# A conv-FFN layer on one core: gelu and gating product through a PSUM bank

## The chip, the cores and the metric

The kernel runs on one core of a Trainium2 chip. A core has a matrix engine (TensorE, PE in the rows), three engines for elementwise work (VectorE, DVE; ScalarE, ACT; GpSimd, POOL), and SyncE (SP), which here issues the DMAs. All working data lie in SBUF; matmul results go to PSUM, eight banks of 128 partitions x 512 fp32 values. TensorE, VectorE and ScalarE reach PSUM in this kernel; GpSimd works on SBUF alone. The metric is device time of one execution in microseconds, as a median of runs.

## The reference

One layer of a hybrid diffusion backbone, in fp32, for 512 latent tokens of width 1024. A token mixer comes first (retention, pooling, gates, output projection, layer norm); the change is in the second half, a gated MLP with a 3x3 depthwise convolution over the 8 x 64 token grid:

```
h = (u @ w_up)                       # 1024 -> 2 x 2816
h = depthwise_conv3x3(h) + conv_b    # over the 8 x 64 grid, per channel
a, b = split(h)                      # 2816 channels each
out = (gelu(a) * b) @ w_down         # 2816 -> 1024
x = post_norm(alpha * x + g2 * out)
```

## The kernel before

Every fp32 matmul operand is split into a high half (a rounded fp32r copy, by ScalarE) and a low half (the operand minus that copy, `sub`, L84, by VectorE or GpSimd), and each product is three matmuls: high x low, high x high, low x high (`mm3`, L93 to L96).

**Up projection.** The 2 x 2816 channels are 44 features of 128 channels, the two halves interleaved, so that feature 2f is the 128 channels of `a` and feature 2f + 1 those of `b` that they are multiplied with: 22 pairs. The loop at L1000 goes over the features. A feature is 8 x 3 = 24 matmuls of 512 columns into one PSUM bank (`feature_mm`, L383). For the first six features the first half of the tokens has been multiplied earlier, while the stage before was ending (`first_half`, L887), so that six banks are taken at the start. The weights of feature i + 2 are loaded and split while feature i is worked on (`up_prep`, L953): the high half by a ScalarE cast, the low half by GpSimd. There are three sets of buffers for them: two of `hi`, `lo`, and every third feature (i % 3 = 2) uses `spare`, parts of the slots that will hold the activations; such matmuls print `ps<-S,S`, the others `ps<-S,hi` and `ps<-S,lo`.

A finished feature is then convolved into an accumulator in SBUF (`accs[i]`, one of eight `t2` buffers). ScalarE writes bias and centre tap from the bank (L1010). Two of the other eight taps are scaled by ScalarE (L1013) and added by GpSimd (L936). The other six are done by VectorE, one instruction each, which reads the bank, the accumulator and a scale per partition (L938); three of feature i are woven with the last three of feature i - 1 (L1015 to L1018). The last two features are first copied out of their banks (L1005).

When both features of a pair are done, ScalarE applies the gelu in place (`gelu`, L983), VectorE multiplies with the other accumulator in place (`gated`, L986), ScalarE casts the product to its high half and VectorE subtracts for the low half (`act_out`, L989). All of these read and write SBUF. The halves are kept for the down projection.

**Down projection.** It runs over f = 0 to 21, each f being 24 matmuls, and accumulates four token blocks x two halves in all eight PSUM banks (`banks`, L1031). The first two f are done on six banks first (L1045). Weights are split as before; the low halves of f = 1 and of every second later f, f = 3 among them, are VectorE's (`down_prep`, L958). When it is done, gates, residual and norm follow.

**What sets the order.** From L922 on SyncE's instructions stay in the written order. For the other engines a planner orders the instructions, by its own estimate of times and by their place in the program, and gives each tile a free buffer of its kind as its use begins; a buffer comes free with the last instruction that uses it. On the chip each engine works through its list in order and waits for semaphores. The PSUM banks are one pool of eight (`bank`, L80).

Of the kernel before, what the change touches and what calls it, by code (L numbers as in the profile page):

```python
# [9 lines left out]
F32 = mybir.dt.float32  # L10
F32R = mybir.dt.float32r
AF = mybir.ActivationFunctionType
ALU = mybir.AluOpType
# [9 lines left out]
NFF = 2816 // P  # L23
# [23 lines left out]
def layer_kernel(ctx: ExitStack, tc: tile.TileContext, a: dict):  # L47
    nc = tc.nc
    act, dve, pool, pe, dma = nc.scalar, nc.vector, nc.gpsimd, nc.tensor, nc.sync
# [7 lines left out]
    def nm(s):  # L57
        count[0] += 1
        return f"{s}_{count[0]}"

    def slot(i, shape, dt=F32):
        return sb.tile(shape, dt, tag=f"S{i}", name=nm(f"S{i}"))
# [17 lines left out]
    def bank():  # L80
        return ps_pool.tile([P, SEQ], F32, tag="ps", name=nm("ps"))

    def sub(eng, out, x, y):
        eng.tensor_tensor(out, x, y, ALU.subtract)  # L84
# [839 lines left out]
    acts = [slot(s, [P, 8, SEQ], F32R) for s in (2, 7, 6, 5, 3, 0)]  # L924
# [44 lines left out]
    srcs, accs = {}, {}  # L969
# [6 lines left out]
    def weave(*gens):  # L976
        gens = list(gens)
        while gens:
            for g in list(gens):
                if next(g, 0) == 0:  # L980
                    gens.remove(g)

    def gelu(f):  # L983
        act.activation(accs[2 * f], accs[2 * f], AF.Gelu_apprx_tanh)

    def gated(f):  # L986
        dve.tensor_tensor(accs[2 * f], accs[2 * f], accs[2 * f + 1], ALU.mult)  # L987

    def act_out(f):  # L989
        hi = acts[f // 8][:, f % 8, :]  # L990
        act.copy(hi, accs[2 * f])
        sub(dve, acts[3 + f // 8][:, f % 8, :], accs[2 * f], hi.bitcast(F32))

    def settle(i):
        if i >= 0 and i % 2 == 0:
            gelu(i // 2)
        elif i >= 0:
            gated(i // 2)

    for i in range(2 * NFF):  # L1000
        up_prep(i + 2)
        ps = up_mm(i)
        if i >= 2 * NFF - 2:
            src = t2()
            act.copy(src, ps)  # L1005
        else:
            src = ps
        srcs[i] = src
        acc = accs[i] = t2()
        act.activation(acc, src, AF.Identity, bias=convb[:, i:i + 1], scale=convw[:, i, 4:5])  # L1010
        for n in POOL_TAPS:
            hs = t2()
            act.activation(hs, src, AF.Copy, scale=convw[:, i, n:n + 1])  # L1013
            tap(acc, hs, None, *TAPS[n])
        gens = [conv_taps(i, DVE_TAPS[:3])]  # L1015
        if i:
            gens.insert(0, conv_taps(i - 1, DVE_TAPS[3:]))
        weave(*gens)  # L1018
        settle(i - 1)
        if i >= 3 and i % 2 == 1:  # L1020
            act_out((i - 3) // 2)
    down0 = down_prep(0, pool)
    i = 2 * NFF - 1
    weave(conv_taps(i, DVE_TAPS[3:]))
    settle(i)
    act_out(NFF - 1)

    g2 = load(row(), gates[1:2, :].broadcast_to([P, D]))
# [176 lines left out]
```

## Time and profile before

| | us |
|---|---|
| median of 3 runs | 873.96 |
| lowest, highest run | 870.28, 1165.45 |
| the profiled execution | 874.79 |
| its span, first to last instruction | 873.0 |
| TensorE busy | 821.6 |
| VectorE busy | 624.4 |
| ScalarE busy | 366.2 |
| GpSimd busy | 444.2 |

The median is near the two lower runs. The profile is one execution, of 874.79 us; all rows below come from it, and their times count from the start of its span. Matmuls overlap, so that one lasts longer (0.39 us) than the distance between two starts.

### The profile page before, as it was taken

What the parts mean: (1) busy time and instruction counts of PE and PEld (TensorE: products, weight loads), DVE (VectorE), ACT (ScalarE), POOL (GpSimd) and SP (SyncE); (2) the same over time, 40 slices, a digit from 0 to 9 for tenths busy, and PEclk for the clock granted to TensorE, in tenths of its full rate; (3) what the DMA queues carried; (4) which work ended last, traced back from release to release, by engine and by line L of the source; (5) the groups of instructions that cost most, each with busy time, mean ns of one, the idle gap of its engine ahead of it and who ended that gap; (6) DMA issues with size and microseconds to landing.
All of it is one profiled execution on the core that took longest, in us unless ns stands there. A gap on an engine that the chain in (4) does not pass through costs nothing.

```text
span 873.0 us, 10556 instructions
## 1 busy us (share of the span) xinstructions
PE 821.6 (94%) x3865; PEld 678.5 (78%) x3865; DVE 624.4 (72%) x959; ACT 366.2 (42%) x575; POOL 444.2 (51%) x304
## 2 busy tenths in 40 slices
PE   6889989999999999998998899999999998799993
PEld 4667878778888888887787898888888776688883
DVE  7899996676267773346757769999999999612138
ACT  4434544121444343233335476666655565223200
POOL 4877411121543230113456878899888886212245
PEclk9999999999999999999999999999999999999997
DMA  9932466767221104344503312222222252224202
GB/s 352 345 105 94 127 207 218 236 226 216 72 73 49 50 1 145 100 154 163 196 1 121 121 50 84 86 96 99 96 97 95 75 169 83 87 97 144 73 1 96
DMA packets 33780, 106.94 MB, mean 122 GB/s; under 512 B 4528, under 2 KB 5312, under 8 KB 33728
## 3 DMA queue, kind: packets, MB, share of 16 engines
q1 hardware_dynamic: 33728, 106.27, 35.6%
q8 instruction: 30, 0.49, 0.2%
q14 instruction: 22, 0.18, 0.1%
HBM read 104.14 MB, written 2.11 MB: 122 GB/s over the span
## 4 chain that ended last, share of the span: by engine, by line
PE 40%; DVE 39%; POOL 8%; DMA 6%; issue 5%; ACT 2%; SPq 0%; DVEq 0%; POOLq 0%; ACTq 0%
DVE t L938 19%; PE ps L96 11%; PE ps L95 11%; PE ps L94 11%; DVE S L84 4%; DMA raw<-in_wada 4%; DVE t L987 3%; POOL lo L84 3%; DVE raw L203 2%; DVE lo L84 2%; PE ps L339 1%; POOL S L84 1%; POOL sm L123 1%; PE ps L608 1%; DVE sm L130 1%
## 5 line engine op out<-in xcount | busy, mean ns | idle before, releaser
L96 PE MATMUL ps<-S,lo 128*128 128x512 f32 (+1 forms) x544 | 212.2, 392 | 5.1 <-DVE lo L84 4.7
L94 PE MATMUL ps<-S,hi 128*128 128x512 f32 (+1 forms) x544 | 213.6, 393 | 2.7 <-ACT hi L89 2.7
L95 PE MATMUL ps<-S,hi 128*128 128x512 f32 (+1 forms) x544 | 212.5, 391 | 0.2 <-POOL S L84 0.2
L84 POOL TENSOR_TENSOR lo<-raw,hi 128x1024 fp32r<-128x1024 f32 (+1 forms) x53 | 134.0, 2530 | 107.2 <-ACT hi L89 105.3
L938 DVE SCALAR_TENSOR_TENSOR t<-ps,convw,t 128x441 f32<-128x441 f32 (+1 forms) x252 | 167.6, 693 | 15.8 <-POOL t L936 11.5
L89 ACT CAST hi<-raw 128x1024 fp32r<-128x1024 f32 (+1 forms) x98 | 98.9, 1009 | 168.2 <-PE ps L95 61.7
L96 PEld LDWEIGHTS ps<-S,lo 128*128 128x128 f32 x544 | 102.8, 189 | 29.8 <-DVE lo L84 6.8
L94 PEld LDWEIGHTS ps<-S,hi 128*128 128x128 f32 x544 | 103.6, 190 | 23.7 <-ACT hi L89 3.1
L936 POOL TENSOR_TENSOR t<-t,t 128x448 f32<-128x448 f32 x88 | 116.7, 1329 | 10.0 <-ACT t L1013 6.2
L95 PEld LDWEIGHTS ps<-S,hi 128*128 128x128 f32 x544 | 103.7, 191 | 21.3 <-POOL S L84 0.6
L95 PE MATMUL ps<-S,S 128*128 128x512 f32 (+1 forms) x308 | 113.8, 370 | 5.4 <-DVE S L84 5.0
L94 PE MATMUL ps<-S,S 128*128 128x512 f32 (+1 forms) x308 | 113.1, 369 | 3.6 <-DVE t L938 3.6
L96 PE MATMUL ps<-S,S 128*128 128x512 f32 (+1 forms) x308 | 113.8, 370 | 0.2 <-POOL S L84 0.2
L84 DVE TENSOR_TENSOR lo<-raw,hi 128x1024 fp32r<-128x1024 f32 (+1 forms) x47 | 61.4, 1307 | 53.0 <-ACT hi L89 53.0
L84 POOL TENSOR_TENSOR S<-raw,S 128x1024 fp32r<-128x1024 f32 x21 | 50.8, 2423 | 68.7 <-ACT S L735 44.5
L95 PE MATMUL ps<-lo,S 128*128 128x512 f32 x208 | 81.6, 392 | 0.7 <-DVE lo L84 0.6
L96 PE MATMUL ps<-hi,S 128*128 128x512 f32 x208 | 81.3, 391 | 0.0
L94 PE MATMUL ps<-hi,S 128*128 128x512 f32 x208 | 79.2, 392 | 0.0
L95 PEld LDWEIGHTS ps<-S,S 128*128 128x128 f32 x308 | 58.9, 191 | 15.6 <-DVE S L84 5.5
L94 PEld LDWEIGHTS ps<-S,S 128*128 128x128 f32 x308 | 58.6, 191 | 13.6 <-DVE t L938 4.0
L96 PEld LDWEIGHTS ps<-S,S 128*128 128x128 f32 x308 | 58.9, 191 | 10.4 <-POOL S L84 1.1
L84 POOL TENSOR_TENSOR S<-t,S 128x512 fp32r<-128x512 f32 (+1 forms) x29 | 44.8, 1557 | 31.2 <-DVE t L220 11.1
(205 smaller groups left out, 1187.3 us busy)
## 6 DMA issues: line engine op xcount, KB each, us to landing
raw<-in_w_up SPq DMA_DIRECT2D x44, 512.0 KB, 3.3
raw<-in_wada SPq DMA_DIRECT2D x32, 512.0 KB, 4.2
raw<-in_w_down SPq DMA_DIRECT2D x22, 512.0 KB, 3.3
S<-in_wada SPq DMA_DIRECT2D x16, 512.0 KB, 6.8
raw<-in_w_first SPq DMA_DIRECT2D x8, 512.0 KB, 7.4
raw<-in_w_v SPq DMA_DIRECT2D x16, 256.0 KB, 3.3
raw<-in_w_ga SPq DMA_DIRECT2D x8, 512.0 KB, 3.4
raw<-in_w_gb SPq DMA_DIRECT2D x8, 512.0 KB, 3.3
```

The lines of the kernel that those rows point to most:

```text
L84: eng.tensor_tensor(out, x, y, ALU.subtract)
L89: act.copy(hi, raw)
L94: pe.matmul(out, lhsT=sh, rhs=mh, start=first, stop=False)
L95: pe.matmul(out, lhsT=sh, rhs=ml, start=False, stop=False)
L96: pe.matmul(out, lhsT=sl, rhs=mh, start=False, stop=last)
L123: pool.tensor_scalar(rs, mv[:, 1:2], EPS, None, ALU.add)
L130: dve.bn_stats(st[:, hf, :], src[:, hf * SEQ:(hf + 1) * SEQ])
L203: dve.scalar_tensor_tensor(out_junk, raw, 1.0, silu_c, ALU.mult, ALU.mult, accum_out=mod[:, j:j + 1])
L339: pe.matmul(g0[f], lhsT=w[:, f * P:(f + 1) * P], rhs=m[:, kt, :], start=kt == 0 and i == 0, stop=kt == NKT - 1 and i == 2)
L936: pool.tensor_tensor(o, o, i, ALU.add)
L938: dve.scalar_tensor_tensor(o, i, w, o, ALU.mult, ALU.add)
L987: dve.tensor_tensor(accs[2 * f], accs[2 * f], accs[2 * f + 1], ALU.mult)
```

## The change

The gelu writes its result to a PSUM bank, not back to the accumulator in SBUF; the product is formed in place in that bank; the cast and the subtraction read it there. The last pair keeps its accumulator in SBUF. Nothing else is changed.

```diff
+    prod = {}
+
     def gelu(f):
-        act.activation(accs[2 * f], accs[2 * f], AF.Gelu_apprx_tanh)
+        prod[f] = accs[2 * f] if f == NFF - 1 else bank()
+        act.activation(prod[f], accs[2 * f], AF.Gelu_apprx_tanh)
 
     def gated(f):
-        dve.tensor_tensor(accs[2 * f], accs[2 * f], accs[2 * f + 1], ALU.mult)
+        dve.tensor_tensor(prod[f], prod[f], accs[2 * f + 1], ALU.mult)
 
     def act_out(f):
         hi = acts[f // 8][:, f % 8, :]
-        act.copy(hi, accs[2 * f])
-        sub(dve, acts[3 + f // 8][:, f % 8, :], accs[2 * f], hi.bitcast(F32))
+        act.copy(hi, prod[f])
+        sub(dve, acts[3 + f // 8][:, f % 8, :], prod[f], hi.bitcast(F32))
```

## Rows read from the trace of the kernel before

**Rows 1.** The page: busy time by engine; the chain that ended last, by line.

```profile
PE 821.6 (94%) x3865; PEld 678.5 (78%) x3865; DVE 624.4 (72%) x959; ACT 366.2 (42%) x575; POOL 444.2 (51%) x304
...
DVE t L938 19%; PE ps L96 11%; PE ps L95 11%; PE ps L94 11%; DVE S L84 4%; DMA raw<-in_wada 4%; DVE t L987 3%; POOL lo L84 3%; DVE raw L203 2%; DVE lo L84 2%; PE ps L339 1%; POOL S L84 1%; POOL sm L123 1%; PE ps L608 1%; DVE sm L130 1%
```

**Rows 2.** Stretches: length, busy us (x starts) of PE, PEld, DVE, ACT, POOL; clock, DMA.

```profile
720.30:732.00 11.70, 8.97 (x37) 6.42 (x35) 11.28 (x16) 5.46 (x8) 8.31 (x6) 1.00 0.27 90
732.00:743.70 11.70, 10.42 (x39) 8.44 (x40) 11.49 (x13) 6.64 (x10) 7.63 (x5) 0.85 0.27 91
743.70:755.40 11.70, 6.66 (x27) 5.00 (x26) 11.10 (x13) 2.84 (x4) 2.43 (x1) 0.95 0.00 0
```

**Rows 3.** Timeline, TensorE: start, us, line, operation; in brackets idle before, releaser.

```profile
527.66 0.39 PE L94 MATMUL ps<-S,S 128*128 128x512 f32 x1
...
674.54 0.39 PE L94 MATMUL ps<-S,S 128*128 128x512 f32 x1
...
726.11 0.39 PE L94 MATMUL ps<-S,S 128*128 128x512 f32 x1
...
733.28 0.50 PE L94 MATMUL ps<-S,S 128*128 128x512 f32 x1 [3.62 <-DVE t L938]
...
754.50 0.80 PE L95 MATMUL ps<-S,S 128*128 128x512 f32 x1 [5.04 <-DVE S L84]
...
761.10 0.39 PE L94 MATMUL ps<-hi,S 128*128 128x512 f32 x1
```

**Rows 4.** Timeline, VectorE: early, one steady pair, the end.

```profile
536.52 0.68 DVE L987 TENSOR_TENSOR t<-t,t 128x512 f32<-128x512 f32 x1
...
616.17 5.66 DVE L938 SCALAR_TENSOR_TENSOR t<-ps,convw,t 128x441 f32<-128x441 f32 x8
621.93 1.38 DVE L987 TENSOR_TENSOR t<-t,t 128x512 f32<-128x512 f32 x1
623.23 2.94 DVE L938 SCALAR_TENSOR_TENSOR t<-ps,convw,t 128x441 f32<-128x441 f32 x4
626.08 1.87 DVE L84 TENSOR_TENSOR S<-t,S 128x512 fp32r<-128x512 f32 x1
627.87 2.67 DVE L938 SCALAR_TENSOR_TENSOR t<-ps,convw,t 128x441 f32<-128x441 f32 x4
...
753.23 1.22 DVE L84 TENSOR_TENSOR S<-raw,S 128x1024 fp32r<-128x1024 f32 x1
754.37 0.68 DVE L987 TENSOR_TENSOR t<-t,t 128x512 f32<-128x512 f32 x1
```

**Rows 5.** Timeline, GpSimd: in the steady pair, and near the end.

```profile
624.99 2.41 POOL L84 TENSOR_TENSOR lo<-raw,hi 128x1024 fp32r<-128x1024 f32 x1 [0.67 <-ACT hi L89]
627.35 2.85 POOL L936 TENSOR_TENSOR t<-t,t 128x448 f32<-128x448 f32 x2
...
735.34 2.38 POOL L936 TENSOR_TENSOR t<-t,t 128x448 f32<-128x448 f32 x2 [5.86 <-ACT t L1013]
```

**Rows 6.** VectorE by line (count | busy us, mean ns | idle): 505-757, then whole.

```profile
L84 DVE TENSOR_TENSOR S<-t,S 128x512 fp32r<-128x512 f32 x22 | 33.7, 1530 | 0.7 <-ACT S L991 0.7
L987 DVE TENSOR_TENSOR t<-t,t 128x512 f32<-128x512 f32 x22 | 29.1, 1324 | 1.3
...
L743 DVE TENSOR_TENSOR S<-ps,S 128x512 f32<-128x512 f32 x8 | 5.5, 691 | 14.7 <-PE ps L96 14.7
...
L84 DVE TENSOR_TENSOR t<-t,t 128x512 fp32r<-128x512 f32 x4 | 2.7, 684 | 0.0
```

**Rows 7.** The same view, ScalarE, 490 to 770 us.

```profile
L1010 ACT ACTIVATE t<-ps,convb,convw 128x512 f32<-128x512 f32 x42 | 32.5, 773 | 3.3 <-PE ps L96 3.3
...
L984 ACT ACTIVATE t<-t 128x512 f32<-128x512 f32 x22 | 13.9, 634 | 43.2 <-DVE t L938 43.2
L991 ACT CAST S<-t 128x512 fp32r<-128x512 f32 x22 | 13.7, 622 | 51.1 <-DVE t L987 51.1
...
L1005 ACT COPY t<-ps 128x512 f32<-128x512 f32 x2 | 1.2, 576 | 0.0
```

## The prediction

> **What bounds the kernel now.** I read the page first, then the table of stretches, then TensorE's timeline, then VectorE's and GpSimd's. The page shows TensorE busy for 94% of the span, but the chain that ended last spends 19% of the span on VectorE's taps at L938 [rows 1]: both engines are near a limit, in different stages. Single stretches tell where. In 720 to 755 us, the end of the up projection and the start of the down projection, TensorE is busy 8.97, 10.42 and 6.66 us of 11.70, starts 37, 39 and 27 matmuls, and its granted clock falls to 0.85 and 0.95; VectorE is busy at least 11.10 of 11.70 in all three [rows 2].
>
> TensorE's own timeline gives its rate and its loss. Features are told apart by their weights: every third (8, 11, 14, ...) has weights in the spare slots and prints `ps<-S,S`. Feature 8 begins at 527.66 and feature 35 at 674.54: 27 features of 24 matmuls in 146.88 us, 0.2267 us each and 5.44 us a feature, with no wait in them [rows 3]. From feature 35 to the down projection's f = 4 (761.10) there are 9 x 24 + 4 x 24 = 312 matmuls, which at that rate take 70.7 us; the rows show 86.6. So **TensorE loses 15.8 us** there, and this is all that a faster up projection can give back: from 527 to 674 it waits for nothing, and behind 761 the change touches nothing. [...]
>
> That pace: one pair of features costs VectorE eight taps, the product, four taps and the low-half subtraction, with no gap; from 616.17 to the next group at 627.87 (1.79 us after the subtraction began) is 11.70 us [rows 4]. TensorE needs 2 x 5.44 = 10.88. VectorE falls 0.8 us a pair behind, and at the end it pays: its last product starts at 754.37 [rows 4], while TensorE finished the up projection at 726.11 [rows 3].
>
> **What the change does, part by part.**
>
> The product and the subtraction. Today both read two SBUF operands: 1.38 and 1.87 us in the steady pair, but 0.68 us for the same product at 754.37 [rows 4], when GpSimd has nothing to do. The wait is for GpSimd: the subtraction begun at 626.08 ends at 627.95, 0.6 us after GpSimd's next instruction could begin (627.35), and GpSimd's two taps take 2.85 us there against 2.38 with nothing in their way at 735.34 [rows 5]. The taps read one operand from PSUM and one from SBUF and keep 0.72 us apart whatever GpSimd does [rows 4]. So an operand in PSUM should end the wait on both sides. Price of the subtraction after: no row has this exact form; the nearest are 0.684 us (two SBUF operands, undisturbed) and 0.691 us (a bank and SBUF, L743, same size) [rows 6]; I take 0.69, upper bound today's mean 1.53. The product writes its result to the bank as well; nothing but TensorE writes PSUM in this trace, so its bounds are 0.69 and today's mean 1.32; I take 0.69, since its reads are those of L743. Over the phase VectorE saves 33.7 - 22 x 0.69 = 18.5 us on subtractions and 29.1 - 22 x 0.69 = 13.9 us on products [rows 6], 32.4 in all (the last pair, which stays as it is, already costs 0.69). A pair falls from 11.70 to about 9.8 us, under TensorE's 10.88.
>
> [...]
>
> GpSimd. Its pair is two weight subtractions of 2.41 and four taps; the taps fall from 2.85 to 2.38 a pair of them [rows 5], so 9.6 us instead of 10.5. It is hidden under TensorE's 10.88, closely: if its waits for the weight casts stayed, it would be the next to bound a pair, at about 11.
>
> ScalarE. The gelu writes a bank: 0.634 us now, bounds 0.576 (a copy out of a bank) and 0.773 (bias and scale out of a bank); the high-half cast (0.622) reads a bank instead: 0.576 to 0.77 [rows 7]. I take no change; at worst 21 x 0.3 = 6 us, which its 43 and 51 us of waiting ahead of these two lines cover [rows 7]. If that cover went, the bias line behind the gelu would come late, and with it GpSimd's and VectorE's taps.
>
> Buffers. The SBUF accumulator is free some 10 us earlier; nothing waits long for it, so nothing is gained. One PSUM bank of eight is taken from the gelu to the end of the subtraction. No DMA, weight or matmul is added or moved. SyncE keeps its written order; the planner orders the other engines and will plan them anew, which the trace of before cannot show.
>
> **The sum.** VectorE's last work would end at 755.1 - 32.4 = 722.7 us if it never starved. TensorE without waits ends the up projection at 674.54 + 9 x 5.44 = 723.5. So VectorE catches up just as TensorE finishes, and then waits for feature 43: copy 0.58, bias 0.77, one scaled copy of like cost, two GpSimd taps 2.4, nine taps at 0.72, product and subtraction, about 12 us (an estimate from rows 4 to 7): done near 736. TensorE needs f = 3's low half at 723.5 + 72 x 0.2267 = 739.8: in time. [...] I leave 3 us of the 15.8: the product bank of f = 20 and the tap bank of feature 41 come free a few us after 723.5, while the down projection wants all eight banks, and f = 1's low half also stands in VectorE's queue. The profiled execution took 874.79 us (span 873.0), 0.8 above the median of 873.96. 874.8 - 15.8 + 3 = **862 us**.
>
> **Rivals.**
>
> *Early banks.* Feature 9 begins at 527.66 + 5.44 = 533.1, while the second product (features 2 and 3) starts only at 536.52 [rows 3, 4]: features 3 to 9 hold seven of eight banks. A product bank makes eight; if two overlap, TensorE must fall back by one or two features, 5.4 to 10.9 us, less what VectorE's faster start gives: 866 to 872. For: seven are full. Against: VectorE saves 2 to 4 us in exactly these first pairs.
>
> *Slower: the gelu waits for a bank.* ScalarE works in order; a gelu that waits for a bank holds back the weight cast and bias behind it, so GpSimd, VectorE and then TensorE. It decides from 1.85 us a pair on (11.70 - 9.85): then VectorE's gain is gone, and TensorE has lost two features early (10.9) and 0.15 x 11.7 = 1.8 us at the lower clock, as in the stretch from 732 [rows 2]: 874.8 + 12.7 = 887; with longer waits more. Against: in the steady pair the product's bank would be given back (627.95) before the next gelu. [...]
>
> *It doesn't do what it says.* If a product that reads and writes a bank still waits for GpSimd, the subtraction alone saves 18.5 us and most of the gain stays; if neither is freed, 873 to 876. Against: the taps.
>
> *More than I count.* All 15.8 us plus a low run: under 857.
>
> **How the numbers follow.** Forecast (858 to 866) 0.66; early banks 0.12; no effect 0.08; gelu waits 0.09; more 0.05. The range 856 to 874 leaves out about half of "more", half of "no effect" and the slower case, some 0.16. 2% of 873.96, about what such a measurement tells from no change, is 17.5 us: faster means under 856.5, which is 18 us below the profiled run and above the 15.8 that can be had, so 0.06; slower means over 891.4, the far end of the gelu case, 0.04; the rest 0.90.
>
> **What would show it.** Right: product and subtraction near 0.69 us while GpSimd is busy; GpSimd's tap pairs at 2.4; TensorE's matmuls 0.227 us apart through 685 to 760 with no long wait and no fall of the clock; f = 4 of the down projection some 12 us earlier; everything from there as before. Wrong: waits of matmuls on VectorE around 515 to 560; ScalarE's gelu waiting for something other than its last tap; a VectorE pair of 11.7 us still; or f = 3 waiting as now.

## The result: slower by a tenth

The changed kernel takes 967.80 us (median of four runs, 965.47 to 969.16) against 873.96 before: a ratio of 1.108 (95% interval 1.106 to 1.110). The forecast was 862 with a range of 856 to 874, and slower by over 2% had a chance of 0.04. The profiled span is 967.4 us, so 94.4 us more than before.

The page after: busy time by engine, then the chain that ended last by line.

```profile
PE 851.1 (88%) x3865; PEld 691.5 (71%) x3865; DVE 604.1 (62%) x959; ACT 364.6 (38%) x575; POOL 425.8 (44%) x304
...
PE ps L96 10%; PE ps L95 10%; PE ps L94 10%; POOL t L936 8%; POOL lo L84 7%; POOL S L84 4%; DVE t L938 4%; DMA raw<-in_wada 3%; DVE raw L203 2%; DVE lo L84 2%; PE ps L339 1%; POOL sm L123 1%; DVE S L84 1%; PE ps L608 1%; DVE S L226 1%
```

VectorE, ScalarE and GpSimd are each busy for **less** time than before (604.1, 364.6 and 425.8 us against 624.4, 366.2 and 444.2 [rows 1]), and the kernel is slower. What the products and subtractions were to save was saved (the next rows), so the loss is waiting. In the chain GpSimd's lines (taps L936, weight low halves L84) have come in, and VectorE's taps have gone from 19% to 4%.

VectorE and ScalarE by line, 500 to 870 us (count | busy us, mean ns | idle before, releaser), to set beside [rows 6, 7]:

```profile
L990 DVE TENSOR_TENSOR ps<-ps,t 128x512 f32<-128x512 f32 x21 | 14.7, 699 | 1.9
L84 DVE TENSOR_TENSOR S<-ps,S 128x512 fp32r<-128x512 f32 x21 | 14.5, 691 | 12.4 <-ACT S L994 12.4
L987 ACT ACTIVATE ps<-t 128x512 f32<-128x512 f32 x21 | 12.6, 602 | 87.1 <-DVE t L938 87.0
L994 ACT CAST S<-ps 128x512 fp32r<-128x512 f32 x21 | 12.3, 586 | 95.9 <-DVE ps L990 95.9
```

Product and subtraction cost 0.70 and 0.69 us, as predicted. But ScalarE now stands still for 87 us ahead of the gelus and 96 us ahead of the casts, where it was 43 and 51 [rows 7]. No gelu waits for a bank: all of its wait is for VectorE's last tap of its own pair.

One pair of features after, ScalarE, then GpSimd, then VectorE (start, us, line, operation; in brackets the idle time before, and its releaser):

```profile
616.09 0.59 ACT L994 CAST S<-ps 128x512 fp32r<-128x512 f32 x1 [4.81 <-DVE ps L990]
616.57 1.05 ACT L89 CAST hi<-raw 128x1024 fp32r<-128x1024 f32 x1
...
619.33 1.06 ACT L949 CAST S<-raw 128x1024 fp32r<-128x1024 f32 x1
620.27 0.80 ACT L1013 ACTIVATE t<-ps,convb,convw 128x512 f32<-128x512 f32 x1
...
626.88 0.60 ACT L987 ACTIVATE ps<-t 128x512 f32<-128x512 f32 x1 [4.65 <-DVE t L938]
632.33 0.58 ACT L994 CAST S<-ps 128x512 fp32r<-128x512 f32 x1 [4.85 <-DVE ps L990]
```

```profile
617.70 2.36 POOL L84 TENSOR_TENSOR lo<-raw,hi 128x1024 fp32r<-128x1024 f32 x1 [6.86 <-ACT hi L89]
620.02 2.37 POOL L936 TENSOR_TENSOR t<-t,t 128x448 f32<-128x448 f32 x2
622.33 2.41 POOL L84 TENSOR_TENSOR S<-raw,S 128x1024 fp32r<-128x1024 f32 x1
624.68 2.41 POOL L936 TENSOR_TENSOR t<-t,t 128x448 f32<-128x448 f32 x2
```

```profile
531.12 0.69 DVE L990 TENSOR_TENSOR ps<-ps,t 128x512 f32<-128x512 f32 x1
...
622.41 4.37 DVE L938 SCALAR_TENSOR_TENSOR t<-ps,convw,t 128x441 f32<-128x441 f32 x6 [5.01 <-POOL t L936]
627.12 4.37 DVE L938 SCALAR_TENSOR_TENSOR t<-ps,convw,t 128x441 f32<-128x441 f32 x6 [0.34 <-POOL t L936]
631.60 0.70 DVE L990 TENSOR_TENSOR ps<-ps,t 128x512 f32<-128x512 f32 x1
...
848.55 0.69 DVE L990 TENSOR_TENSOR t<-t,t 128x512 f32<-128x512 f32 x1
```

Read the three together, by starts. The cast of one product (616.09) is followed by the next pair's first weight cast (+0.48), GpSimd's low half (+1.13), its taps (+2.32), the second low half (+2.31), the second taps (+2.35), VectorE's last six taps (+2.44), the product (+4.48) and the next cast (+0.73): 632.33. **The pair is one serial chain of 16.24 us**, in which each engine waits for the one before. In the kernel before, VectorE had no gap in 11.70 us [rows 4].

That is the whole loss. From the second product to the last there are 20 pairs: 848.55 - 531.12 = 317.4 us, against 754.37 - 536.52 = 217.9 us [rows 4]. The 99.6 us between them, less the 5.40 us by which the second product is earlier, is 94.2. TensorE shows the same 94.2 us at the wait for f = 3's low half, which is still there (848.69 now, 754.50 [rows 3]). TensorE's timeline after:

```profile
520.93 0.77 PE L94 MATMUL ps<-S,hi 128*128 128x512 f32 x1 [4.27 <-DVE t L938]
521.49 0.63 PE L95 MATMUL ps<-S,hi 128*128 128x512 f32 x1
521.92 0.63 PE L96 MATMUL ps<-S,lo 128*128 128x512 f32 x1
...
633.91 0.50 PE L94 MATMUL ps<-S,hi 128*128 128x512 f32 x1 [1.71 <-ACT hi L89]
...
636.35 0.50 PE L96 MATMUL ps<-S,lo 128*128 128x512 f32 x1 [1.70 <-POOL lo L84]
...
848.69 0.79 PE L95 MATMUL ps<-S,S 128*128 128x512 f32 x1 [5.21 <-DVE S L84]
```

One early wait for a bank costs 4.27 us. After that the waits are for weight halves, late because ScalarE casts the next weights only behind the product's cast. Behind the wait at 520.93 the matmuls start 0.43 us apart instead of 0.227, about half the rate, and the granted clock of a stretch as long as the old pair is 0.87, where the kernel before has 1.00 over 500 to 720 us (columns as in [rows 2]):

```profile
611.00:622.70 11.70, 9.52 (x36) 7.20 (x35) 5.75 (x9) 6.42 (x10) 4.92 (x4) 0.87 0.12 44
```

**What changed is the order on ScalarE.** The view by line of ScalarE, from 480 us to just ahead of a gelu, counts what stands ahead of it. Before, up to 617.5 us (the gelu of 617.58 comes next), and after, up to 626.8 us (the gelu of 626.88 comes next):

```profile
L1010 ACT ACTIVATE t<-ps,convb,convw 128x512 f32<-128x512 f32 x23 | 17.8, 774 | 3.3 <-PE ps L96 3.3
L984 ACT ACTIVATE t<-t 128x512 f32<-128x512 f32 x10 | 6.3, 633 | 10.8 <-DVE t L938 10.8
```

```profile
L1013 ACT ACTIVATE t<-ps,convb,convw 128x512 f32<-128x512 f32 x18 | 14.2, 789 | 3.3 <-PE ps L96 3.3
L987 ACT ACTIVATE ps<-t 128x512 f32<-128x512 f32 x8 | 4.8, 602 | 26.4 <-DVE t L938 26.4
```

Before, the eleventh gelu comes behind 23 biases; its own pair and those ahead of it are 22 features, so one feature of the next pair has been started. By the cast of its product it is two (one more bias follows the gelu). I call this the **lead**, as gelu/cast: 1/2 before. After, the ninth gelu comes behind 18 biases, which is its own pair and nothing more, and no bias comes between it and its cast: 0/0. So GpSimd and VectorE have nothing of the next pair to do while ScalarE waits for this one. Counted in this way at every pair, the lead before falls from 4/5 at the first pair to 1/2 at the seventh and stays there until the last two; after, it is 4/4 and 2/2 at the first two pairs and 0/0 from the third on.

### The profile page after: what moved, and what is told of

The parts are those of the page before. It is cut to its first block, busy times and chain, and to the rows that moved or that the text cites. A ratio compares the mean times of both kernels' runs of the same rounds, so it can differ in the third digit from the quotient of the medians.

```text
span 967.4 us, 10561 instructions
## 1 busy us (share of the span) xinstructions
PE 851.1 (88%) x3865; PEld 691.5 (71%) x3865; DVE 604.1 (62%) x959; ACT 364.6 (38%) x575; POOL 425.8 (44%) x304
## 4 chain that ended last, share of the span: by engine, by line
PE 36%; POOL 22%; issue 18%; DVE 16%; DMA 5%; ACT 2%; POOLq 0%; SPq 0%; DVEq 0%; ACTq 0%
PE ps L96 10%; PE ps L95 10%; PE ps L94 10%; POOL t L936 8%; POOL lo L84 7%; POOL S L84 4%; DVE t L938 4%; DMA raw<-in_wada 3%; DVE raw L203 2%; DVE lo L84 2%; PE ps L339 1%; POOL sm L123 1%; DVE S L84 1%; PE ps L608 1%; DVE S L226 1%
## 5 line engine op out<-in xcount | busy, mean ns | idle before, releaser
L938 DVE SCALAR_TENSOR_TENSOR t<-ps,convw,t 128x441 f32<-128x441 f32 (+1 forms) x252 | 173.3, 698 | 113.9 <-POOL t L936 107.5
L94 PE MATMUL ps<-S,hi 128*128 128x512 f32 (+1 forms) x544 | 220.4, 405 | 23.6 <-ACT hi L89 19.3
L96 PE MATMUL ps<-S,lo 128*128 128x512 f32 (+1 forms) x544 | 218.9, 404 | 24.5 <-POOL lo L84 18.7
L95 PE MATMUL ps<-S,hi 128*128 128x512 f32 (+1 forms) x544 | 217.8, 400 | 0.5 <-POOL S L84 0.5
L84 POOL TENSOR_TENSOR lo<-raw,hi 128x1024 fp32r<-128x1024 f32 (+1 forms) x53 | 130.9, 2470 | 181.9 <-ACT hi L89 179.9
L96 PEld LDWEIGHTS ps<-S,lo 128*128 128x128 f32 x544 | 106.9, 197 | 54.0 <-POOL lo L84 23.5
L94 PEld LDWEIGHTS ps<-S,hi 128*128 128x128 f32 x544 | 106.8, 196 | 49.9 <-ACT hi L89 24.4
L94 PE MATMUL ps<-S,S 128*128 128x512 f32 (+1 forms) x308 | 117.1, 382 | 17.4 <-ACT S L949 15.6
L96 PE MATMUL ps<-S,S 128*128 128x512 f32 (+1 forms) x308 | 117.2, 381 | 9.7 <-POOL S L84 9.7
L95 PEld LDWEIGHTS ps<-S,hi 128*128 128x128 f32 x544 | 106.8, 196 | 22.5 <-POOL S L84 0.7
L95 PE MATMUL ps<-S,S 128*128 128x512 f32 (+1 forms) x308 | 116.2, 378 | 5.2 <-DVE S L84 5.2
L936 POOL TENSOR_TENSOR t<-t,t 128x448 f32<-128x448 f32 x88 | 101.9, 1161 | 12.4 <-ACT t L1016 9.1
L84 POOL TENSOR_TENSOR S<-raw,S 128x1024 fp32r<-128x1024 f32 x21 | 50.4, 2403 | 105.7 <-ACT S L949 60.2
L84 DVE TENSOR_TENSOR lo<-raw,hi 128x1024 fp32r<-128x1024 f32 (+1 forms) x47 | 61.4, 1307 | 53.5 <-ACT hi L89 53.4
L94 PEld LDWEIGHTS ps<-S,S 128*128 128x128 f32 x308 | 60.6, 197 | 30.6 <-ACT S L949 18.5
L96 PEld LDWEIGHTS ps<-S,S 128*128 128x128 f32 x308 | 60.7, 197 | 22.5 <-POOL S L84 12.6
L95 PEld LDWEIGHTS ps<-S,S 128*128 128x128 f32 x308 | 60.7, 197 | 15.3 <-DVE S L84 5.5
L84 POOL TENSOR_TENSOR S<-t,S 128x512 fp32r<-128x512 f32 (+1 forms) x29 | 45.0, 1563 | 30.7 <-DVE t L220 11.1
```

Of the source, the lines that this page charges most:

```text
L94: pe.matmul(out, lhsT=sh, rhs=mh, start=first, stop=False)
L95: pe.matmul(out, lhsT=sh, rhs=ml, start=False, stop=False)
L96: pe.matmul(out, lhsT=sl, rhs=mh, start=False, stop=last)
L936: pool.tensor_tensor(o, o, i, ALU.add)
L938: dve.scalar_tensor_tensor(o, i, w, o, ALU.mult, ALU.add)
```

## The experiments

Three explanations were to be told apart: the request for a bank inside the loop makes the planner lose the lead (the plan); eight banks are too few, on the chip; or the new instructions are slow. Ratios are to the kernel before, timed again in the same session as each experiment (medians of 874.37, 875.28 and 874.00 us), with 95% intervals. All lines numbered 980 and above shift by a few between kernels.

**gate.** The kernel before, all operands in SBUF as they were, with one tiny copy into a bank that nobody reads.

```diff
         act.activation(accs[2 * f], accs[2 * f], AF.Gelu_apprx_tanh)
+        if f < NFF - 1:
+            act.copy(bank()[:, 0:1], accs[2 * f][:, 0:1])
```

> The kernel before, gelu, product and subtraction all in SBUF; only a bank is asked for right behind each gelu, ScalarE copies one column into it, and it is free again at once. Theory 1 (the request): the planner hands out banks in the order of the program, so the bank of the next pair's first feature cannot be planned before the gelu; the plan loses its lead of one to two features, and the engines' lists become one serial chain per pair. Then this kernel is as slow as the changed one, 950 to 985 us, about 16 us a pair in place of 11.7. Theory 2 (too few banks): the bank is held for a fraction of a us, so 874 to 880. Theory 3 (work in PSUM is slow or collides): nothing but one column is in PSUM, 874 to 880.

Measured: 971.67 us, 1.112 (1.109 to 1.115). ScalarE's waits, 505 to 850 us (who waits, for whom: us in total, times, longest):

```profile
ACT S L993 <- DVE t L989: 96.6, 22, 5.4
ACT t L984 <- DVE t L938: 93.3, 21, 6.5
```

The copies themselves take 0.16 us each, 3.4 us in all. The request alone brings the whole loss, with waits close to those after, and the counts ahead of its ninth gelu are again 18 biases and 8 gelus; at every pair the lead is that of the changed kernel. No operand in PSUM is needed for it.

**static2.** The change, with two banks taken once ahead of the loop and used in turn.

```diff
     prod = {}
+    pbank = [bank() for _ in range(2)]
...
-        prod[f] = accs[2 * f] if f == NFF - 1 else bank()
+        prod[f] = accs[2 * f] if f == NFF - 1 else pbank[f % 2]
```

> The changed kernel, but the products use two banks asked for once, ahead of the loop, in turn; six are left for features all the time. Theory 1: with no request inside the loop the plan keeps its lead, product and subtraction cost 0.69 us, and the gain that was forecast appears: 857 to 866 us. Theory 2: two banks are taken for good, more than in the changed kernel: 960 us or more. Theory 3: the same work in PSUM as in the changed kernel: about 968.

Measured: 863.47 us, 0.988 (0.986 to 0.991). The operands of the change, without its requests inside the loop, are faster than before by 10.9 us, about what was forecast for it. VectorE's steady pair:

```profile
619.49 0.70 DVE L991 TENSOR_TENSOR ps<-ps,t 128x512 f32<-128x512 f32 x1
620.45 2.94 DVE L938 SCALAR_TENSOR_TENSOR t<-ps,convw,t 128x441 f32<-128x441 f32 x4 [0.27 <-POOL t L936]
623.36 0.69 DVE L84 TENSOR_TENSOR S<-ps,S 128x512 fp32r<-128x512 f32 x1
623.97 1.38 DVE L938 SCALAR_TENSOR_TENSOR t<-ps,convw,t 128x441 f32<-128x441 f32 x2
625.89 4.37 DVE L938 SCALAR_TENSOR_TENSOR t<-ps,convw,t 128x441 f32<-128x441 f32 x6 [0.55 <-POOL t L936]
630.37 0.70 DVE L991 TENSOR_TENSOR ps<-ps,t 128x512 f32<-128x512 f32 x1
```

From product to product it is 10.88 us, TensorE's own pace of 2 x 5.44. In 500 to 720 us TensorE's clock stays full, while the changed kernel has 0.91 (static2, then the changed kernel):

```profile
500.00:720.00 220.00, 216.93 (x1027) 181.96 (x1027) 189.08 (x282) 136.65 (x202) 182.74 (x120) 1.00 0.29 98
```

```profile
500.00:720.00 220.00, 176.68 (x748) 140.44 (x749) 133.38 (x197) 97.06 (x144) 124.56 (x84) 0.91 0.18 61
```

**hold2.** The kernel before with two more banks asked for ahead of the loop. They were to be held, unused, to feature 40.

```diff
+    held_b = [bank() for _ in range(2)]
+    for t in held_b:
+        act.copy(t[:, 0:1], convb[:, 0:1])
     for i in range(2 * NFF):
+        if i == 2 * NFF - 4:
+            for t in held_b:
+                act.copy(small([P, 1]), t[:, 0:1])
```

> The kernel before with two banks taken out of use from the start of the up projection's loop to its 40th feature, by a one-column copy into each at the start and out of each at the end; gelu, product and subtraction stay in SBUF. Theory 1: the order of the lists stays, 872 to 880 us (early on TensorE may wait a few us for a bank). Theory 2: banks are what is short, 930 us or more. Theory 3: 874.

Measured: 875.09 us, 1.001 (1.000 to 1.003). **The run doesn't hold the banks.** The copies out of them are written at feature 40, but the planner set them right behind the copies in (ScalarE's timeline; L1002 writes the banks, L1006 reads them):

```profile
493.51 0.15 ACT L1002 COPY ps<-convb 128x1 f32<-128x1 f32 x1
...
494.23 0.16 ACT L1002 COPY ps<-convb 128x1 f32<-128x1 f32 x1
494.33 0.26 ACT L1006 COPY sm<-ps 128x1 f32<-128x1 f32 x2
```

The banks were in use for about 1 us, before the loop's first bias at 503.59, so this run doesn't test whether six banks are enough. It shows that two short requests ahead of the loop change nothing: the lead is that of before at every pair. "Too few banks" is ruled out by others: in gate the extra bank is in use for 0.16 us at a time and the whole loss is there; in static2 two banks belong to the products from the first gelus to the last but one pair, so that six are left for the features, and the loop runs at TensorE's pace; and no gelu waits for a bank.

**mmahead.** The change as it is, with a bank asked for at each gelu, but the matmuls (and so their requests for banks) written two features earlier in the program.

```diff
+    pss = {i: up_mm(i) for i in range(2)}
     for i in range(2 * NFF):
-        up_prep(i + 2)
-        ps = up_mm(i)
+        up_prep(i + 4)
+        if i + 2 < 2 * NFF:
+            pss[i + 2] = up_mm(i + 2)
+        ps = pss.pop(i)
```

> The changed kernel with a bank asked for at every gelu as before, but the matmuls of a feature (and the loading of its weights) are written two features earlier in the program, so that the banks of the next pair are asked for ahead of the gelu's. Theory 1 (what counts is the place of the request in the program): the lead comes back, 858 to 868 us. Rival: any bank asked for inside the loop upsets the plan, wherever it stands: 950 us or more.

Measured: 861.82 us, 0.985 (0.983 to 0.988), with products 10.88 us apart as in static2. The requests stay; the matmuls' own requests, and with them the loading and splitting of the weights, now stand ahead of them in the program (the run doesn't part these two). At every gelu and cast the lead is that of static2. So it is the place that counts: as the change writes it, features 2f + 2 and later ask for their banks behind gelu f, and the lists no longer have them ahead of it.

**mid4.** The change for four pairs only.

```diff
-        prod[f] = accs[2 * f] if f == NFF - 1 else bank()
+        prod[f] = bank() if 8 <= f < 12 else accs[2 * f]
```

> The change in four pairs alone (f = 8 to 11), the rest as before. Theory 1 as a cost per pair: 4 x (16.2 - 11.7) = 18 us more, 885 to 897 us, the pairs behind them back at 11.7. Rival: the lead is lost once at the first request and does not come back: 930 us or more. Rival: only the requests while the first banks are taken do harm: 870 to 876 us.

Measured: 880.08 us, 1.006 (1.004 to 1.008). A miss in size: less was lost than expected. The four pairs do take 16.2 us each (6-tap groups at 618.45 and 634.72), but the pairs behind them are faster than the old 11.70:

```profile
618.45 4.37 DVE L938 SCALAR_TENSOR_TENSOR t<-ps,convw,t 128x441 f32<-128x441 f32 x6 [5.05 <-POOL t L936]
...
634.72 4.37 DVE L938 SCALAR_TENSOR_TENSOR t<-ps,convw,t 128x441 f32<-128x441 f32 x6 [5.02 <-POOL t L936]
...
670.51 0.69 DVE L990 TENSOR_TENSOR t<-t,t 128x512 f32<-128x512 f32 x1
673.98 1.17 DVE L84 TENSOR_TENSOR S<-t,S 128x512 fp32r<-128x512 f32 x1
...
680.83 0.69 DVE L990 TENSOR_TENSOR t<-t,t 128x512 f32<-128x512 f32 x1
```

These pairs come 10.3 us apart, with a product of 0.69 and a subtraction of 1.17 us on two SBUF operands, not 1.38 and 1.87 [rows 4]. So part of the loss is won back. That GpSimd and VectorE meet at other points of the pair behind the disturbance would explain it; no run tests this alone. Counted as above, the lead is 0/0 at the four pairs, 0/2 at the next and then 1/2: it returns as soon as no bank is asked for.

**static1 and static1f.** One fixed bank. In static1 gelu f is written ahead of the cast and subtraction of pair f - 1, so with one bank these read the next pair's values; its time stands for the same work in another order. In static1f they are written first.

```diff
+    pbank = [bank()]
...
-        prod[f] = accs[2 * f] if f == NFF - 1 else bank()
+        prod[f] = accs[2 * f] if f == NFF - 1 else pbank[0]
...
-        settle(i - 1)
         if i >= 3 and i % 2 == 1:
             act_out((i - 3) // 2)
+        settle(i - 1)
```

(static1 has the first two parts, static1f all three.)

> As with two banks, but one bank for all products; the gelu of a pair then waits for the subtraction of the pair before it. Theory 1: the lead stays, 857 to 868 us, a little behind two banks if VectorE waits for the gelu between subtraction and product (some 0.5 us a pair, hidden under TensorE's 10.88). Theory 2: better than two banks, near or below 968. Theory 3: about 968.

> One fixed bank for all products, asked for ahead of the loop, with the cast and subtraction of a pair written ahead of the next pair's gelu, so that one bank is enough. The first pairs keep more lead than with two fixed banks. Theory 1: 857 to 862 us, TensorE with less than 2 us of waits from 499 to 760 where two fixed banks have 4.7. If the gelu's wait for the subtraction hurts: 866 us or more.

Measured: static1 859.06 us, 0.983 (0.981 to 0.986); static1f 860.57 us, 0.983 (0.981 to 0.986), with a span of 857.6. static1f is faster than both kernels and has the lowest median of the versions with the right values, but mmahead's interval overlaps its own. In 500 to 720 us its TensorE has no gap:

```profile
500.00:720.00 220.00, 220.00 (x1041) 185.13 (x1040) 191.97 (x288) 139.10 (x207) 186.66 (x122) 1.00 0.30 100
```

**wr_a, wr_b, wr_late: the lead without a planner.** In the up projection all of SyncE, ScalarE, VectorE and GpSimd keep the written order. wr_a is the change so ordered, wr_b the kernel before so ordered (no bank is asked for), and wr_late the change so ordered with the gelu moved behind the bias of the next pair's first feature, where the product already stands in the written order.

```diff
-    ordered(*ORD3)
+    ordered(E_SP, E_ACT, E_DVE, E_POOL)
...
+    ordered(*ORD3)
     down0 = down_prep(0, pool)
```

```diff
-        settle(i - 1)
+        if i >= 2 and i % 2 == 0:
+            gelu(i // 2 - 1)
+            gated(i // 2 - 1)
```

(The second part is wr_late's alone, with the last pair's gelu and product written behind the loop.)

> The changed kernel, bank requests untouched, but ScalarE, VectorE and GpSimd keep the order of the program in the up projection's loop, in which the cast of a pair's product stands behind the next pair's biases and scaled copies. Theory 1 says that the request does its harm only through the order of the lists: 858 to 876 us. Rival: on the chip itself something waits for the product's bank: 930 us or more.

> The kernel before, no bank asked for, with ScalarE, VectorE and GpSimd in the order of the program; its gelu stands right behind its own pair's biases, one feature earlier than in the plan of before. Theory 1 (the lists' lead alone decides): as slow as the changed kernel in written order (934), 920 to 945 us, some 14 us a pair. Rival (the product's bank is what is waited for on the chip): 880 us or less.

> The changed kernel in written order, a bank asked for at every gelu, with the gelu written one feature later, behind the bias and scaled copies of the next pair's first feature, so that ScalarE's list has the lead that the plan of before had. Theory 1: 858 to 872 us, though the bank is asked for and held as in the changed kernel. Rival (the bank): 930 us or more.

Measured: wr_a 934.14 us, 1.068 (1.065 to 1.070); wr_b 936.79 us, 1.071 (1.069 to 1.074); wr_late 865.08 us, 0.989 (0.985 to 0.992). **wr_a was a miss**: I had overlooked that in the written order the gelu stands right behind its own pair's bias, too. That miss gave the cleaner test. One gelu of wr_a, one of wr_b, one of wr_late:

```profile
635.48 0.60 ACT L987 ACTIVATE ps<-t 128x512 f32<-128x512 f32 x1 [7.42 <-DVE t L938]
```

```profile
626.16 0.63 ACT L984 ACTIVATE t<-t 128x512 f32<-128x512 f32 x1 [7.79 <-DVE t L938]
```

```profile
616.55 0.61 ACT L987 ACTIVATE ps<-t 128x512 f32<-128x512 f32 x1
```

With a lead of 0/2 (the cast of pair f - 1 follows gelu f, the gelu has no lead) a pair takes 14.1 us in wr_a and 14.5 in wr_b, with the bank and without (the gelus ahead of those shown start at 621.41 and 611.69). With 1/2, in wr_late, the gelu doesn't wait and a pair takes 10.88 (the next gelu starts at 627.43), although a bank is asked for at every gelu. So the time goes with the lead, whether or not a bank is asked for: 0/0 gives 16.2 us a pair, 0/2 14 to 14.5, and 1/2 what the busier engine needs.

**subonly and prodonly: the prices.** Both with two fixed banks. In subonly gelu stays in SBUF, the product reads two SBUF operands and writes the bank. In prodonly gelu goes to the bank and the product back to SBUF.

```diff
-        act.activation(prod[f], accs[2 * f], AF.Gelu_apprx_tanh)
+        act.activation(accs[2 * f], accs[2 * f], AF.Gelu_apprx_tanh)
...
-        dve.tensor_tensor(prod[f], prod[f], accs[2 * f + 1], ALU.mult)
+        dve.tensor_tensor(prod[f], accs[2 * f], accs[2 * f + 1], ALU.mult)
```

```diff
-        dve.tensor_tensor(prod[f], prod[f], accs[2 * f + 1], ALU.mult)
+        dve.tensor_tensor(accs[2 * f], prod[f], accs[2 * f + 1], ALU.mult)
...
-        act.copy(hi, prod[f])
-        sub(dve, acts[3 + f // 8][:, f % 8, :], prod[f], hi.bitcast(F32))
+        act.copy(hi, accs[2 * f])
+        sub(dve, acts[3 + f // 8][:, f % 8, :], accs[2 * f], hi.bitcast(F32))
```

> Two fixed banks, but only the subtraction's operand lies in PSUM: the gelu stays in SBUF, the product reads two SBUF operands and writes the bank. By the price per operation (1.87 to 0.69 us) a pair falls from 11.70 to about 10.5, under TensorE's 10.88: 860 to 867 us, nearly all of the gain. If VectorE's waits for GpSimd only move to the product: 868 us or more.

> Two fixed banks, but only the product's operand lies in PSUM: the gelu writes the bank, the product reads it and writes SBUF, cast and subtraction stay in SBUF. By the price (1.38 to 0.69 us) a pair falls to about 11.0, just over TensorE's 10.88: 862 to 870 us. If the waits only move to the subtraction: 872 us or more.

Measured: subonly 866.63 us, 0.992 (0.990 to 0.993); prodonly 861.98 us, 0.987 (0.984 to 0.989). VectorE by line, 500 to 870 us, subonly and then prodonly:

```profile
L991 DVE TENSOR_TENSOR ps<-t,t 128x512 f32<-128x512 f32 x21 | 24.8, 1183 | 1.8
L84 DVE TENSOR_TENSOR S<-ps,S 128x512 fp32r<-128x512 f32 x21 | 14.3, 682 | 0.7 <-ACT S L995 0.7
```

```profile
L84 DVE TENSOR_TENSOR S<-t,S 128x512 fp32r<-128x512 f32 x22 | 18.4, 837 | 2.9 <-ACT S L995 2.9
L991 DVE TENSOR_TENSOR t<-ps,t 128x512 f32<-128x512 f32 x21 | 14.5, 690 | 1.8
```

With one input in a bank the mean is 682 and 690 ns. With both inputs in SBUF it is longer, 1183 and 837 ns, wherever the instruction writes; but it isn't longer every time: in prodonly 17 of the 22 subtractions take 0.68 to 0.69 us, and GpSimd's taps are the longer ones (1254 ns on the mean, 1166 in subonly). Either half of the change brings a pair to TensorE's 10.9 us. Against 874.00 subonly gains 7.4 us and prodonly 12.0, where both halves gained 10.9 in static2.

## Why the prediction was wrong, by its own steps

**The step that failed** is the last one of the parts, on buffers: "One PSUM bank of eight is taken", and the planner "will plan them anew, which the trace of before cannot show". I named it and left it out of the sum, at nothing. It was worth more than the whole +94 us: gate, which has only this step, loses 97.3 us against the kernel before beside it (874.37), and static2, which has all but this step, gains 10.9. I counted a bank as a place that must be free on the chip. It is also a request at a place in the program: with the request inside the loop, the planner no longer set the next features' work ahead of the gelu. That it is the place of the request is shown by gate, static2 and mmahead; that the planner serves requests of one kind in the order of the program is the reading that fits all twelve runs, not something that a trace shows.

**The cover.** I let 43 and 51 us of ScalarE's waiting cover any change there [rows 7]. That waiting costs nothing only while the next pair's weight cast and bias stand *ahead* of the gelu and the cast. The lead is what made it cover, and it could have been counted from the trace of before: 23 biases ahead of the eleventh gelu. What an order with only part of the lead costs wr_b shows: 62.8 us, with no bank asked for.

**The slower rival** had the right chain (ScalarE in order holds back cast and bias, then GpSimd, VectorE, TensorE) and the wrong trigger: a gelu that waits for a bank. No gelu did. Its price of 887 counted two features of TensorE lost once; the loss came at every pair, 16.24 - 11.70 = 4.5 us some twenty times, far past the 1.85 us from which the rival was to decide.

**Early banks** was true in part: one early wait of 4.27 us, and one of 1.30 us at the same place in static2, both under the 5.4 us at which a single feature's fall-back was priced. With a wait of 1.70 us for a weight's low half at 538.72, static2 is 5.3 us behind the kernel before when feature 11 begins (549.27, against 543.98), 1.2 of them since before 508 us; its lead is 0/1 and 0/2 at the third and fourth pair, where static1f has 3/3 and 2/2.

**The prices** were right. Product 0.699 and subtraction 0.687 us in static2, beside a busy GpSimd, where I took 0.69 for both; GpSimd's tap pairs are at 2.40 there (2.38 taken). In subonly and prodonly VectorE is slower only with two SBUF inputs: 1.18 us against 0.68, and 0.84 against 0.69. That it is GpSimd that holds it up then is my reading of these times; how it would do so no run shows. The changed kernel's own 0.70 and 0.69 prove nothing: gate, with two SBUF inputs, has 691 ns for both, and GpSimd stands still there (in the 6.88 us ahead of 617.93, in which the product of 615.56 and the subtraction of 616.93 fall). A bank as the operand adds nothing that these times show: 0.682 to 0.699 us with a bank, 0.684 without [rows 6].

**ScalarE's durations**, taken as unchanged, became a little shorter: gelu 605 ns (634), cast 589 (622) in static2 [rows 7].

**The sum.** With the lead kept, the cap of 15.8 us held: static2 has a span 10.5 us shorter and a median of 863.47, static1f 15.4 us shorter and 860.57. The 3 us that the sum left were put in the wrong place. Two matmuls of static2, the first of feature 11 and the first of the down projection's f = 4 (761.10 before [rows 3]):

```profile
549.27 0.39 PE L94 MATMUL ps<-S,S 128*128 128x512 f32 x1
...
750.58 0.39 PE L94 MATMUL ps<-hi,S 128*128 128x512 f32 x1
```

The 201.3 us between them are 33 features and four f at 0.2267 us a matmul, without a wait: the end gave back all of the 15.8, and what static2 lost it lost early. So that 862 lies close to 863.47 is in part luck. "Done near 736" was too early as well (the 755.1 it rests on leaves out the last pair's subtraction, at 755.73 before). In static1f VectorE's low half of f = 3 runs from 740.01 to 741.23, when TensorE has been at f = 3 since 740.27; it costs nothing because five matmuls that don't need it stand first in the list.

## What to carry to other kernels

Where a planner orders the engines, a new request for a buffer inside a pipelined loop can be an edit of the order, not only of the buffer count: take such buffers once ahead of the loop, or write the request behind those of the work that has to run ahead. Before pricing an edit at an engine that waits, count in the trace how many later items it has started ahead of that wait; this lead is the cover, and a plan without it costs the whole chain of a pair. When the engines for elementwise work get less busy and the kernel gets slower, look for a changed order first, by counting two lines up to the same event in both traces.

## What the runs showed that was not expected

- A copy of one column, 0.16 us on ScalarE and read by nobody, makes the kernel 97.3 us slower, because it asks for a bank inside the loop.
- The same subtraction on two SBUF operands takes 1.87 us in the steady pair before [rows 4], 1.17 in mid4 behind the disturbance, 0.69 in gate, where GpSimd stands still, and 0.68 to 1.68 in prodonly. That this depends on where VectorE and GpSimd meet in a pair is my reading, which no run tests alone. The mean of one line in one kernel is not a price for another.
- With two banks given to the products, six are left for the features, and the loop still runs at TensorE's pace (static2, 863.47 us).
